# Copies inside SBUF issued from three queues by kind, the compressing products with split weights and blocks, and another order of the forget attention's projections

## The chip, the cores and the metric

One core of one Trainium2 chip runs one program, two transformer blocks one after the other. The metric is the device time of an execution in microseconds (us), as the median of several. In the text PE is TensorE, DVE VectorE, ACT ScalarE, POOL GpSimd and SP SyncE; the last three also issue DMAs, each from a queue of its own that is served in order.

## The reference, cut to what matters

512 tokens of width 1024, float32. The first block has forget attention and gated linear attention side by side, cross attention and an MLP; the second has a SwiGLU, differential attention beside a sparse attention (NSA), and another SwiGLU. What the change touches:

```python
# block 1: fq, fk, fv, ff (forget attention), gq, gk, gv, glr, gr (gated linear attention)
proj = xn @ w_in
fq, fk = rms_norm(fq per head, g_q), rms_norm(fk per head, g_k)
log_f = log_sigmoid(ff + b); c = cumsum(log_f)
p = softmax(fq.fk/8 + c_t - c_s, causal); fox_out = p @ fv
# block 2: rotary embedding on q and k of the differential attention, on q and two k of NSA
apply_rope: [x1*cos - x2*sin, x2*cos + x1*sin]
# compress(x_raw, pos, w1, w2), once for keys and once for values
blocks = x_raw[31 blocks of 32 tokens, stride 16] + pos      # (31, 2 groups, 32*64)
return gelu(blocks @ w1) @ w2                                # w1: 2048 x 256, w2: 256 x 64
```

## The kernel before, in words

Everything stands feature by token in SBUF. To keep float32 accuracy in single-pass products, a float32 matrix is split into a rounded part h (ACT, `act`, L154) and the rest l (DVE, `lo`, L148); a product is then h by h, h by l and l by h. Weights come from HBM on SP's queue into a ring of three tiles `wraw`, and are split into a ring of four tiles `wspl` (`wsub`, L176 on); `lin` makes a 512-token projection out of 24 products, `nat` one with the tokens on the partitions out of 96 products with 256 columns. The results go to PSUM tiles `lin`, of which the attention stages have three.

The score products read keys and queries twice side by side: `dup` copies the h part of the keys into a tile `kd` and the l part into `kl` (four copies of 64x512 each), and `stacks` puts h and l of the queries into `qu` (two copies of h, two of l). Such a copy is a DMA inside SBUF, `move` (L371). `rope` (L434) swaps halves of 32 partitions by four DMAs of 32x512 into a tile `tb`. In the kernel before all of them are issued from POOL's queue, where POOL's own operations also stand.

Each stage is a pair of generators, an attention and a filler (the projections that it still needs), which `weave` interleaves by the time of the products that each has issued; `pipe` lets several projections of a filler overlap, so that one goes on where another yields `LATER`. The order inside an engine is then set by the build's scheduler, by its own times. In the forget attention (`fox`, scores of 8 heads; `fox_in`) the filler was the list `[gates(), key(0), query(0), value(0), key(1), query(1), value(1)]`, and after it `gla_proj(0)`, projections of the gated linear attention. `gates()` holds the log-sigmoids, with four loads of ACT's function table, and the cumulated sums.

`cmp_in(i)` makes the blocks for the compression: a projection, four shifted copies on POOL's queue into a `wraw` tile, and two additions of the positions (DVE) into a tile `nsv`. `compress(i)` streams the weights cw1 through four `wraw` tiles and multiplies them in float32: 64 products over the two calls, 128 weights' columns by 64 columns of blocks. A float32 product is two matmul records in the trace.

Of the kernel before, what the change touches and what calls it, by code (L numbers as in the profile page):

```python
# [122 lines left out]
class Net:  # L123
    def __init__(self, tc, a, dbg=None):
        self.tc, self.nc, self.a = tc, tc.nc, a
        self.dbg = dbg or (lambda *x: None)
        self.mark = lambda n: None
        self.tb = {"d": 1}
        self.lag = 2
        self.groups = [[0], [1, 3], [2]]  # L130
        self.foxp = [None] * 4
        self.foxs = 0
        self.foxvok = [False, False]
        self.dap = [None] * 8
# [247 lines left out]
    def dup(self, t, U):  # L382

        for j in range(2):
            for r in range(2):
                self.move(U[r * 64:(r + 1) * 64, j], t[j * 64:(j + 1) * 64])
        return U
# [158 lines left out]
    def mixer(self):  # L546
# [74 lines left out]
    def fox_in(self, X, rb, rn, p1, p2, y, gate, first):  # L621
# [37 lines left out]
        K = {}  # L659

        def key(g):
            def done(t, ps):
                kh, kl = self.R(), self.R()
                self.scaled_split(ps, self.gcol("foxk"), kh, kl)
                K[2 * g + t] = [self.dup(z, p2.tile([128, 2, 512], F32R, name=n)) for z, n in ((kh, "kd"), (kl, "kl"))]
            yield from self.head_tiles(a["n_fqk"][2 + g], X, rn, p1, lambda t: self.foxs >= 2 * (2 * g + t) - 2, done,
                                       None if g else first)
# [14 lines left out]
        yield from pipe([gates(), key(0), query(0), value(0), key(1), query(1), value(1)])  # L682
# [302 lines left out]
    def mix2(self, hctx, densepsum):  # L985
# [4 lines left out]
        with ExitStack() as r0:  # L990
            with ExitStack() as l0:
                z = None
                with ExitStack() as r1:
                    with ExitStack() as l1:
# [6 lines left out]
                        with ExitStack() as c:  # L1001
# [12 lines left out]

                            def fill():
                                self.N = {}
                                pieces = [[self.nsa_key(0, X, rb, n1)], [self.nsa_key(1, X, rb, n1)],
# [100 lines left out]
    def da_key(self, h, X, rb, p2):  # L1118
# [8 lines left out]
        self.dak[h] = [self.dup(t, p2.tile([128, 2, 512], F32R, name=n)) for t, n in zip(z, ("kd", "kl"))]  # L1127
# [119 lines left out]
    def nsa_key(self, b, X, rb, p1):  # L1247
# [8 lines left out]
        for U, t in zip(self.N["kb"], (kh, kl)):  # L1256
            self.dup(t, U[:, b])
# [170 lines left out]
    def cmp_in(self, i, X, rb, p1):  # L1428

        nc, a = self.nc, self.a  # L1430
        p2 = self.tmp
        ps = yield from self.lin(a["t_c4"][i], X)
        k0 = self.T("a")
        self.tt(k0, ps, rb, OP.mult)

        B = p1.tile([128, 4, 2, 2, 2, 64], F32R, name="nsv") if i == 0 else self.Bt
        self.Bt = B
        B = B.rearrange("p a b c d e -> p (a b c d e)").bitcast(F32)[:, i * 1024:(i + 1) * 1024]
        B = B.rearrange("p (k g n) -> p k g n", k=16, g=2)
        nc.gpsimd.memset(B, 0.0)  # L1440
        pos = p2.tile([128, 16], F32, name="cpos", bufs=1)
        nc.sync.dma_start(pos, a["cpos"][i])
        sh = self.wraw.tile([128, 1024], F32, name="wraw").rearrange("p (g n) -> p g n", g=2)
        for g in range(2):
            nc.gpsimd.dma_start(sh[0:64, g], k0[64 * g:64 * g + 64])
            nc.gpsimd.dma_start(sh[64:128, g, 0:511], k0[64 * g:64 * g + 64, 1:512])
        yield LATER
        for g in range(2):

            v = bass.AP(tensor=sh.tensor, offset=sh[:, g].offset, ap=[list(sh.ap[0]), [2, 16], [16, 31]])  # L1450
            self.tt(B[:, :, g, 0:31], v, pos[:, :, None].to_broadcast([128, 16, 31]), OP.add)
        self.B = B

    def compress(self, i, p1):
# [3 lines left out]
        if True:  # L1458
            pc = None
            for c in range(4):  # L1460
                w = self.wraw.tile([128, 1024], F32, name="wraw")
                w3 = w.rearrange("p (k n) -> p k n", k=4)
                nc.sync.dma_start(w3, a["cw1"][i][:, 4 * c:4 * c + 4])
                yield LATER
                if pc is None:
                    B = self.B
                    pc = self.ps()
                    pss = [pc[:, :64], pc[:, 64:128]]
# [8 lines left out]
            nc.vector.tensor_copy(x, pc[:, :128])  # L1477
# [9 lines left out]
            r = 4 if i else 1  # L1487
            H = p2.tile([128, 2, 2, r, 32], F32, name=f"ch{i}", bufs=1)
            for m in range(2):
                self.tt(H[:, m], *(z[:, 64 * m:64 * m + 64].rearrange("p (g n) -> p g n", g=2)[:, :, None]  # L1490
                                   .to_broadcast([128, 2, r, 32]) for z in (x, u)), OP.mult)
            w2 = p2.tile([128, 2, 128], F32, name="cw2", bufs=1)
            nc.sync.dma_start(w2, a["cw2"][i])
            yield LATER
            if i == 0:
                ps = self.ps()
                for m in range(2):
                    self.mm(ps[:, :64], w2[:, m], H[:, m, :, 0], m == 0, m == 1)
# [6 lines left out]
            else:  # L1505
# [3 lines left out]
                for g in range(2):  # L1509
                    ps = self.ps()  # L1510
                    for m in range(2):
                        self.mm(ps[:, :64], H[:, m, g].rearrange("p r n -> p (r n)"), w2[:, m, :64], m == 0, m == 1)
# [173 lines left out]
```

## Time and profile before

| | |
|---|---|
| median of 3 runs | 2279.53 us (2278.78 to 2280.15) |
| profiled execution | 2278.2 us, its span 2276.4 us |
| PE busy | 2222.3 us (98%) |
| DVE, ACT, POOL busy | 1278.6, 967.3, 371.2 us (56%, 42%, 16%) |
| mean granted clock of PE | 0.983 |
| DMA mean, HBM read | 100 GB/s, 188.91 MB |

The profile describes one execution. Times are counted from the start of its span; 1.8 us of the execution lie outside it. PE is never far from busy, so what a change can win are the stretches where PE waits, and those where its granted clock is at the lower of its two levels (1.2 GHz instead of 2.4 GHz: 0.5 in the profile). The views by stretch of time show both side by side.

### The profile page before, as it was taken

The numbers are of one execution on the slowest core, as the hardware profiler recorded it, in microseconds if no ns is written. First come the engines' busy times: TensorE is split into PE (matmuls) and PEld (weight loads), VectorE is DVE, ScalarE is ACT, GpSimd is POOL, SyncE is SP. The second block draws the span as 40 slices with busy tenths as digits, with TensorE's granted clock in tenths as the row PEclk, the third lists the DMA queues.
The fourth block names the chain that finished last, engine by engine and source line by source line (L and its number), as shares of the span: only waits on it lengthen the run. The fifth ranks groups of instructions, "written<-read, shape, count | busy, mean of one in ns | idle before, by whom it ended". The sixth has DMA issues, their size and how long they took to land. (4 is left out here: it accounts for less than half of the span.)

```text
span 2276.4 us, 30717 instructions
## 1 busy us (share of the span) xinstructions
PE 2222.3 (98%) x11491; PEld 1867.7 (82%) x11491; DVE 1278.6 (56%) x2403; ACT 967.3 (42%) x1941; POOL 371.2 (16%) x569
## 2 busy tenths in 40 slices
PE   9999999999999999999999899999999999999998
PEld 8887799888888888888887788788877888888887
DVE  6565566654345444434456667778784555543543
ACT  6553455444234333323343244466675334332332
POOL 1431012100000000000005345445651000000000
PEclk9999999999999999999999899999999999999999
DMA  3441243233333333233345655512212333333322
GB/s 134 112 121 52 75 122 108 63 95 96 96 99 94 101 93 96 89 104 101 101 137 142 168 165 153 147 43 66 63 45 65 112 102 93 94 91 104 102 88 79
DMA packets 75108, 228.13 MB, mean 100 GB/s; under 512 B 12560, under 2 KB 20464, under 8 KB 74960
## 3 DMA queue, kind: packets, MB, share of 16 engines
q1 hardware_dynamic: 61392, 192.48, 27.9%
q0 software_dynamic: 12992, 33.18, 5.6%
q8 instruction: 90, 1.47, 0.3%
q14 instruction: 58, 0.48, 0.1%
q10 hardware_dynamic: 576, 0.52, 0.1%
HBM read 188.91 MB, written 4.19 MB: 85 GB/s over the span
## 5 line engine op out<-in xcount | busy, mean ns | idle before, releaser
L154 ACT ACTIVATE wspl<-wraw 128x512 fp32r<-128x512 f32 (+1 forms) x677 | 422.3, 627 | 877.6 <-PE lin L145 800.3
L148 DVE TENSOR_TENSOR wspl<-wraw,wspl 128x512 fp32r<-128x512 f32 (+1 forms) x677 | 470.0, 697 | 428.0 <-ACT wspl L154 420.8
L244 POOL TENSOR_TENSOR rqr<-rqv,mhalf 128x4 f32<-128x4 f32 (+1 forms) x21 | 20.5, 977 | 1369.2 <-DVE rqv L241 1358.6
L145 PE MATMUL lin<-x0h,wspl 128*128 128x512 f32 (+2 forms) x396 | 158.1, 400 | 2.2 <-DVE h L151 0.9
L154 ACT ACTIVATE P<-s,nm 128x128 f32<-128x128 f32 (+2 forms) x224 | 117.5, 529 | 86.1 <-DVE nm L316 73.8
L145 PE MATMUL lin<-x1h,wspl 128*128 128x512 f32 (+2 forms) x396 | 153.6, 389 | 0.0
L145 PE MATMUL lin<-x7h,wspl 128*128 128x512 f32 (+2 forms) x396 | 153.5, 388 | 0.0
L145 PE MATMUL lin<-x2h,wspl 128*128 128x512 f32 (+2 forms) x396 | 153.5, 388 | 0.0
L145 PE MATMUL lin<-x3h,wspl 128*128 128x512 f32 (+2 forms) x396 | 153.2, 388 | 0.0
L145 PE MATMUL lin<-x4h,wspl 128*128 128x512 f32 (+2 forms) x396 | 153.0, 387 | 0.0
L145 PE MATMUL lin<-x6h,wspl 128*128 128x512 f32 (+2 forms) x396 | 152.9, 387 | 0.0
L145 PE MATMUL lin<-x5h,wspl 128*128 128x512 f32 (+2 forms) x396 | 152.7, 386 | 0.0
L316 DVE TENSOR_REDUCE nm<-s 128x1 f32<-128x128 f32 (+3 forms) x208 | 105.3, 510 | 38.7 <-PE s L145 37.7
L148 DVE TENSOR_TENSOR ptl<-tr,pth 128x512 fp32r<-128x512 f32 x152 | 88.2, 597 | 19.8 <-ACT pth L154 18.6
L154 ACT ACTIVATE pth<-tr 128x512 fp32r<-128x512 f32 x152 | 74.8, 530 | 39.6 <-PE tr L342 34.6
L145 PEld LDWEIGHTS lin<-x0h,wspl 128*128 128x128 f32 (+1 forms) x396 | 75.3, 190 | 17.5 <-ACT wspl L154 3.5
L342 PE MATMUL tr<-ident,P 128*128 128x128 f32 x480 | 83.1, 283 | 4.8 <-DVE P L151 3.5
L145 PEld LDWEIGHTS lin<-x2h,wspl 128*128 128x128 f32 (+1 forms) x396 | 74.7, 189 | 15.3
L145 PEld LDWEIGHTS lin<-x1h,wspl 128*128 128x128 f32 (+1 forms) x396 | 74.9, 189 | 14.8
L145 PEld LDWEIGHTS lin<-x3h,wspl 128*128 128x128 f32 (+1 forms) x396 | 74.4, 188 | 15.2
L145 PEld LDWEIGHTS lin<-x7h,wspl 128*128 128x128 f32 (+1 forms) x396 | 74.5, 188 | 15.0 <-issue 0.3
L145 PEld LDWEIGHTS lin<-x4h,wspl 128*128 128x128 f32 (+1 forms) x396 | 74.4, 188 | 14.8
(707 smaller groups left out, 5673.2 us busy)
## 6 DMA issues: line engine op xcount, KB each, us to landing
wraw<-in_t_m SPq DMA_DIRECT2D x64, 512.0 KB, 3.8
wraw<-in_t_f1a SPq DMA_DIRECT2D x22, 512.0 KB, 3.6
wraw<-in_t_f1b SPq DMA_DIRECT2D x22, 512.0 KB, 3.5
wraw<-in_t_f2a SPq DMA_DIRECT2D x22, 512.0 KB, 3.5
wraw<-in_t_f2b SPq DMA_DIRECT2D x22, 512.0 KB, 3.5
qu<-r POOLq DMA_DIRECT2D x80, 128.0 KB, 3.1
wraw<-in_t_f1c SPq DMA_DIRECT2D x16, 512.0 KB, 3.5
wraw<-in_t_f2c SPq DMA_DIRECT2D x16, 512.0 KB, 3.5
```

The costliest lines, as they stand in the source:

```text
L145: self.nc.tensor.matmul(out, lhsT, rhs, start=start, stop=stop, **kw)
L148: self.nc.vector.tensor_tensor(out, in0, in1, op=op)
L154: self.nc.scalar.activation(out, in_, func, **kw)
L244: self.nc.gpsimd.tensor_tensor(r, v, self.mhalf[:, :m], op=OP.pow)
L316: self.nc.vector.tensor_reduce(nm, ps, axis=AX.X, op=OP.max, negate=True)
L342: self.nc.tensor.transpose(ps[:, n:n + 128], P(qb, kb) if callable(P) else P[:, self.po(qb) + kb * 128:self.po(qb) + (kb + 1) * 128], self ...
```

## The change

It does four things. `move` and `rope` get a queue by kind: copies of an h part are issued from ACT, copies of an l part from POOL as before, and the four copies of a `rope` from SP (96, 104 and 104 of the 304). The blocks of the compression are split into h and l, and its weights run through `wsub` like all others: 64 products with 128 columns (h weights by h and l of the blocks) and 64 with 64 columns (l by h), one matmul record each, and 16 more splits on ACT and DVE; the shifted copies go into tiles `tb` instead of `wraw`. In the forget attention's filler `key(0)` stands ahead of `gates()`, and `gla_proj(0)` behind `value(0)` instead of at the end. The two tiles `cpos` and `cw2` are loaded earlier, the repeated hidden vector is copied by POOL (two operations).

```diff
+        self.q = {"hi": self.nc.scalar, "lo": self.nc.gpsimd, "rope": self.nc.sync}
...
-    def move(self, dst, src):
-        self.nc.gpsimd.dma_start(dst.bitcast(F32), src.bitcast(F32))
+    def move(self, dst, src, q="lo"):
+        self.q[q].dma_start(dst.bitcast(F32), src.bitcast(F32))
...
-        self.move(U[0:64, 0], hi[0:64])
+        self.move(U[0:64, 0], hi[0:64], "hi")
         self.move(U[64:128, 0], lo[0:64])
         self.move(U[0:64, 1], lo[64:128])
-        self.move(U[64:128, 1], hi[64:128])
+        self.move(U[64:128, 1], hi[64:128], "hi")
...
         for q in range(4):
-            self.nc.gpsimd.dma_start(sw[q * 32:(q + 1) * 32], src[(q ^ 1) * 32:(q ^ 1) * 32 + 32])
+            self.q["rope"].dma_start(sw[q * 32:(q + 1) * 32], src[(q ^ 1) * 32:(q ^ 1) * 32 + 32])
...
-                yield from self.fox_in(X, rb, rn, p1, p2, y, gates, first)
-                yield from self.gla_proj(0, X, rb, rn, p0)
+                yield from self.fox_in(X, rb, rn, p1, p2, y, gates, first, self.gla_proj(0, X, rb, rn, p0))
...
-        yield from pipe([gates(), key(0), query(0), value(0), key(1), query(1), value(1)])
+        yield from pipe([key(0), gates(), query(0), value(0), other, key(1), query(1), value(1)])
...
+            t = self.T("c").rearrange("p (k n) -> p k n", k=16)
+            nc.vector.memset(t[:, :, 31:32], 0.0)
+            self.tt(t[:, :, 0:31], v, pos[:, :, None].to_broadcast([128, 16, 31]), OP.add)
+            self.act(B[:, :, 0, g], t, AF.Copy)
+            self.lo(B[:, :, 1, g], t, B[:, :, 0, g])
...
             for c in range(4):
-                w = self.wraw.tile([128, 1024], F32, name="wraw")
-                w3 = w.rearrange("p (k n) -> p k n", k=4)
-                nc.sync.dma_start(w3, a["cw1"][i][:, 4 * c:4 * c + 4])
-                yield LATER
+                W = self.wsub(a["cw1"][i][:, 4 * c:4 * c + 4])
...
-                for k in range(4):
+                for k, (h, l) in enumerate(W):
                     for m in range(2):
-                        self.mm(pss[m], w3[:, k, m * 128:(m + 1) * 128],
-                                B[:, 4 * c + k].rearrange("p g n -> p (g n)"),
-                                c + k + m == 0, c + k == 6, skip_group_check=True)
-                yield 8 * 213
+                        w, o = slice(128 * m, 128 * m + 128), 128 * m
+                        self.mm(pc[:, o:o + 128], h[:, w], B[:, 4 * c + k], c + k + m == 0, False,
+                                skip_group_check=True)
+                        self.mm(pc[:, o:o + 64], l[:, w], B[:, 4 * c + k, :64], False, c + k == 6,
+                                skip_group_check=True)
+                yield 8 * 110
```

Three places show how the order moves. Line numbers of the changed kernel are 2 higher at these helpers. **Start of the forget attention, ACT**, from the narrow gate rows on (`tc`, `td` and `cm` belong to `gates()`; `hraw` and `tb` empty a PSUM tile of `query(0)`). Before:

```order
L154 ACTIVATE tc<-tc 8x512
L154 ACTIVATE td<-s,gc 128x512
L154 ACT_TABLE_LOAD
L154 ACTIVATE tc<-tc 8x512
L154 ACTIVATE tc<-s,gc 128x512
L154 ACT_TABLE_LOAD
L154 ACTIVATE td<-td 128x512
L154 ACTIVATE tc<-tc 128x512
L154 ACT_TABLE_LOAD
L154 ACTIVATE td<-td 128x512
L154 ACTIVATE tc<-tc 128x512
L154 ACTIVATE cm<-ta 8x512
```

and now:

```order
L156 ACTIVATE tc<-tc 8x512
L156 ACT_TABLE_LOAD
L156 ACTIVATE tc<-tc 8x512
L156 ACTIVATE hraw<-lin 128x256
L156 ACTIVATE tb<-lin 128x256
L156 ACTIVATE hraw<-lin 128x256
```

One table load instead of three, and 2 other rows instead of 9, stand between the narrow gate row and the emptying of `query(0)`'s tiles; the other loads now stand among the tiles of `value(0)`, together with 8 copies of the h part of the keys.

**Start of the differential attention, PE**, at the first score products (`kd`, `kl`, `qu` of head 0). Before, behind the projection of `cmp_in(0)`:

```order
L145 MATMUL lin<-x7h,wspl 128x512
L145 MATMUL lin<-x7l,wspl 128x512
L145 MATMUL lin<-x7h,wspl 128x512
L145 MATMUL s<-kd,qu 128x128
L145 MATMUL s<-kl,qu 128x128
```

and now, after 12 products of the first `da_value`:

```order
L147 MATMUL lin<-wspl,x2h 128x256
L147 MATMUL lin<-wspl,x3h 128x256
L147 MATMUL s<-kd,qu 128x128
L147 MATMUL s<-kl,qu 128x128
L147 LDWEIGHTS identb
L147 MATMUL s<-maskb,identb 128x128
L147 MATMUL lin<-wspl,x3l 128x256
```

The first scores moved ahead of 84 products with 256 columns and 24 with 512, and the following ones lie between those products.

**The same place, SP.** Before:

```order
L180 DMA wraw<-in_t_kda 128x1024
L180 DMA wraw<-in_t_qda 128x1024
L180 DMA wraw<-in_n_vda 128x1024 x2
L180 DMA wraw<-in_t_c 128x1024
L1463 DMA wraw<-in_cw 128x1024
L180 DMA wraw<-in_t_c 128x1024
```

and now:

```order
L182 DMA wraw<-in_t_qda 128x1024
L182 DMA wraw<-in_n_vda 128x1024
L436 DMA tb<-ta 32x512 x8
L182 DMA wraw<-in_n_vda 128x1024
L436 DMA tb<-ta 32x512 x8
L182 DMA wraw<-in_t_c 128x1024
L182 DMA wraw<-in_cw 128x1024
L436 DMA tb<-ta 32x512 x8
L182 DMA wraw<-in_t_c 128x1024
```

The copies of six `rope` stand between the loads of weights that set SP's pace.

## Rows read from the trace of the kernel before

**Rows 1.** The page: busy time of the engines; the groups of weight splits.
```profile
PE 2222.3 (98%) x11491; PEld 1867.7 (82%) x11491; DVE 1278.6 (56%) x2403; ACT 967.3 (42%) x1941; POOL 371.2 (16%) x569
...
L154 ACT ACTIVATE wspl<-wraw 128x512 fp32r<-128x512 f32 (+1 forms) x677 | 422.3, 627 | 877.6 <-PE lin L145 800.3
L148 DVE TENSOR_TENSOR wspl<-wraw,wspl 128x512 fp32r<-128x512 f32 (+1 forms) x677 | 470.0, 697 | 428.0 <-ACT wspl L154 420.8
```
**Rows 2.** By stretch: us, busy of PE, PEld, DVE, ACT, POOL, granted clock, DMA.
```profile
35.00:85.00 50.00, 41.02 (x286) 38.22 (x284) 26.61 (x56) 24.52 (x55) 21.36 (x32) 0.83 0.43 111
1235.00:1285.00 50.00, 39.44 (x175) 30.98 (x175) 30.39 (x61) 15.50 (x42) 23.57 (x44) 0.80 0.57 159
1285.00:1325.00 40.00, 36.25 (x198) 28.23 (x197) 28.69 (x63) 14.58 (x38) 15.91 (x26) 0.91 0.58 158
1425.00:1485.00 60.00, 55.41 (x319) 46.58 (x318) 43.20 (x98) 29.20 (x79) 22.31 (x40) 0.94 0.48 131
1485.00:1675.00 190.00, 189.13 (x1131) 157.79 (x1131) 150.68 (x357) 121.03 (x325) 103.68 (x148) 1.00 0.22 61
1675.00:1717.00 42.00, 37.26 (x225) 29.24 (x224) 33.96 (x86) 28.80 (x85) 24.93 (x40) 0.92 0.09 20
1237.00:1250.00 13.00, 7.77 (x37) 4.61 (x35) 9.07 (x23) 6.46 (x20) 10.25 (x19) 0.84 0.62 171
```
**Rows 3.** Waits of PE from 35 to 85 us: total, times, longest.
```profile
PE s L145 <- DMA qu<-r: 5.4, 1, 5.4
PE lin L145 <- ACT tb L154: 3.4, 1, 3.4
```
**Rows 4.** Timeline of ACT in the gates: start, us, operation.
```profile
29.46 0.71 ACT L154 ACTIVATE tc<-misc,gc 8x512 f32<-8x512 f32 x1
...
31.72 1.28 ACT L154 ACT_TABLE_LOAD   x1
...
41.96 0.38 ACT L154 ACTIVATE tb<-lin 128x256 f32<-128x256 f32 x1 [1.77 <-DVE cs L653]
```
**Rows 5.** Timeline of POOL, the first copies of the forget attention.
```profile
57.98 4.17 POOL L371 DMA_DIRECT2D kd<-r  x8 [4.01 <-ACT r L154]
```
**Rows 6.** Waits of PE from 1235 to 1330 us.
```profile
PE s L145 <- ACT P L154: 2.8, 5, 1.0
PE lin L145 <- issue: 2.8, 1, 2.8
PE s L145 <- DMA qu<-r: 2.7, 1, 2.7
PE lin L145 <- DMA wraw<-in_cw: 2.2, 1, 2.2
```
**Rows 7.** Timeline of POOL at the start of the differential attention.
```profile
1203.71 4.02 POOL L434 DMA_DIRECT2D tb<-ta  x8 [8.79 <-DVE ta L151]
...
1224.87 1.10 POOL L371 DMA_DIRECT2D qu<-r  x2
```
**Rows 8.** A DMA issued on ACT; the page's issues of `qu`, us to landing.
```profile
L1553 ACTq DMA_DIRECT2D outT<-x1h x1: 381/381/381, 2269.3 to 2269.3; - x1
...
qu<-r POOLq DMA_DIRECT2D x80, 128.0 KB, 3.1
```
**Rows 9.** Timeline of PE at compressing and score products of 128 columns.
```profile
1288.44 1.67 PE L145 MATMUL lin<-nsv,wraw 128*128 128x64 f32 x14
1289.93 0.31 PE L145 MATMUL s<-kd,qu 128*128 128x128 f32 x1
1290.07 0.28 PE L145 MATMUL s<-kl,qu 128*128 128x128 f32 x1
```
**Rows 10.** Stretches with one kind of product: 512 columns; 256 columns (PE alone).
```profile
600.00:700.00 100.00, 100.00 (x443) 82.84 (x442) 40.35 (x59) 34.00 (x54) 0.00 (x0) 1.00 0.31 95
...
105.00:110.00 5.00, 5.00 (x43) 1.00 0.34 110
```
**Rows 11.** Timeline of SP: two loads, the second waiting for its buffer.
```profile
1314.73 9.37 SPq L180 DMA_DIRECT2D wraw<-in_n_vda  x2
```

More of the change, by code (lines that the diff above doesn't have):

```diff
@@ L619, in log_sigmoids, with fox_in @@
             yield m
-    def fox_in(self, X, rb, rn, p1, p2, y, gate, first):
+    def fox_in(self, X, rb, rn, p1, p2, y, gate, first, other):
         nc, a = self.nc, self.a
@@ L664, in done @@
                 self.scaled_split(ps, self.gcol("foxk"), kh, kl)
-                K[2 * g + t] = [self.dup(z, p2.tile([128, 2, 512], F32R, name=n)) for z, n in ((kh, "kd"), (kl, "kl"))]
+                K[2 * g + t] = [self.dup(z, p2.tile([128, 2, 512], F32R, name=n), q)
+                                for z, n, q in ((kh, "kd", "hi"), (kl, "kl", "lo"))]
             yield from self.head_tiles(a["n_fqk"][2 + g], X, rn, p1, lambda t: self.foxs >= 2 * (2 * g + t) - 2, done,
@@ L1013, in mix2 @@
                             d1, d2 = self.newpool("da1", 1, c), self.newpool("da2", 2, c)
+                            self.cpos = n1.tile([128, 32], F32, name="cpos")
+                            for i in range(2):
+                                nc.sync.dma_start(self.cpos[:, 16 * i:16 * i + 16], a["cpos"][i])
                             def fill():
                                 self.N = {}
+                                self.B = {}
                                 pieces = [[self.nsa_key(0, X, rb, n1)], [self.nsa_key(1, X, rb, n1)],
@@ L1126, in da_key @@
         z = self.split(k1, p2, "k", hring=True, lring=True)
-        self.dak[h] = [self.dup(t, p2.tile([128, 2, 512], F32R, name=n)) for t, n in zip(z, ("kd", "kl"))]
+        self.dak[h] = [self.dup(t, p2.tile([128, 2, 512], F32R, name=n), q)
+                       for t, n, q in zip(z, ("kd", "kl"), ("hi", "lo"))]
     def da_query(self, h, X, rb, p2):
@@ L1255, in nsa_key @@
             self.N["kb"] = [p1.tile([128, 2, 2, 512], F32R, name="kb" + x) for x in "hl"]
-        for U, t in zip(self.N["kb"], (kh, kl)):
-            self.dup(t, U[:, b])
+        for U, t, q in zip(self.N["kb"], (kh, kl), ("hi", "lo")):
+            self.dup(t, U[:, b], q)
     def nsa_gates(self, X, rb, p1):
@@ L1434, in cmp_in @@
         self.tt(k0, ps, rb, OP.mult)
[L1436 to L1443, printed above, removed]
+        sh = []
         for g in range(2):
-            nc.gpsimd.dma_start(sh[0:64, g], k0[64 * g:64 * g + 64])
-            nc.gpsimd.dma_start(sh[64:128, g, 0:511], k0[64 * g:64 * g + 64, 1:512])
+            t = self.T("b")
+            nc.gpsimd.dma_start(t[0:64], k0[64 * g:64 * g + 64])
+            nc.gpsimd.dma_start(t[64:128, 0:511], k0[64 * g:64 * g + 64, 1:512])
+            sh.append(t)
         yield LATER
+        B = p1.tile([128, 4, 2, 2, 2, 64], F32R, name="nsv")
+        B = B.rearrange("p a b c d e -> p (a b c d e)").rearrange("p (k z g n) -> p k z g n", k=16, z=2, g=2)
+        pos = self.cpos[:, 16 * i:16 * i + 16]
         for g in range(2):
-            v = bass.AP(tensor=sh.tensor, offset=sh[:, g].offset, ap=[list(sh.ap[0]), [2, 16], [16, 31]])
-            self.tt(B[:, :, g, 0:31], v, pos[:, :, None].to_broadcast([128, 16, 31]), OP.add)
-        self.B = B
+            v = bass.AP(tensor=sh[g].tensor, offset=sh[g].offset, ap=[list(sh[g].ap[0]), [2, 16], [16, 31]])
+            t = self.T("c").rearrange("p (k n) -> p k n", k=16)
[3 more added lines that the diff above has]
+            self.lo(B[:, :, 1, g], t, B[:, :, 0, g])
+        self.B[i] = B
     def compress(self, i, p1):
@@ L1458, in compress @@
         if True:
-            pc = None
+            w2 = p2.tile([128, 2, 128], F32, name="cw2", bufs=2)
+            nc.sync.dma_start(w2, a["cw2"][i])
             for c in range(4):
-                w = self.wraw.tile([128, 1024], F32, name="wraw")
-                w3 = w.rearrange("p (k n) -> p k n", k=4)
-                nc.sync.dma_start(w3, a["cw1"][i][:, 4 * c:4 * c + 4])
-                yield LATER
-                if pc is None:
-                    B = self.B
+                W = self.wsub(a["cw1"][i][:, 4 * c:4 * c + 4])
+                if c == 0:
+                    yield LATER
+                    B = self.B[i].rearrange("p k z g n -> p k (z g n)")
                     pc = self.ps()
-                    pss = [pc[:, :64], pc[:, 64:128]]
-                for k in range(4):
+                for k, (h, l) in enumerate(W):
                     for m in range(2):
-                        self.mm(pss[m], w3[:, k, m * 128:(m + 1) * 128],
-                                B[:, 4 * c + k].rearrange("p g n -> p (g n)"),
-                                c + k + m == 0, c + k == 6, skip_group_check=True)
-                yield 8 * 213
+                        w, o = slice(128 * m, 128 * m + 128), 128 * m
[4 more added lines that the diff above has]
+                yield 8 * 110
             yield LATER
             x = p2.tile([128, 128], F32, name="cx", bufs=1)
-            nc.vector.tensor_copy(x, pc[:, :128])
+            pz = pc[:, :256].rearrange("p (m z n) -> p m z n", m=2, z=2)
+            x3 = x.rearrange("p (m n) -> p m n", m=2)
+            self.act(x3, pz[:, :, 1], AF.Copy)
+            self.tt(x3, pz[:, :, 0], x3, OP.add)
             u = p2.tile([128, 128], F32, name="cu", bufs=1)
@@ L1485, in compress @@
             nc.vector.reciprocal(u, u)
[L1487 to L1493, printed above, removed]
+            H = p2.tile([128, 2, 64], F32, name="ch", bufs=1)
+            self.tt(H.rearrange("p m n -> p (m n)"), x, u, OP.mult)
             yield LATER
@@ L1510, in compress @@
                     ps = self.ps()
+                    H4 = p2.tile([128, 2, 4, 32], F32, name="cr", bufs=1)
+                    nc.gpsimd.tensor_copy(H4, H[:, :, None, 32 * g:32 * g + 32].to_broadcast([128, 2, 4, 32]))
                     for m in range(2):
-                        self.mm(ps[:, :64], H[:, m, g].rearrange("p r n -> p (r n)"), w2[:, m, :64], m == 0, m == 1)
+                        self.mm(ps[:, :64], H4[:, m].rearrange("p r n -> p (r n)"), w2[:, m, :64], m == 0, m == 1)
                     for j in range(2):
```

6 lines of the change are left out of this document (3 added, 3 removed).

## The prediction

> **What bounds the kernel now.** The page's busy row first: TensorE (PE) works 2222.3 of 2276.4 us, the next engine, VectorE, 56% [rows 1]. So the change can win only where PE is idle, 54.1 us in all, and where its granted clock lies below 1, the level of 2.4 GHz. I read the view by stretches next, around the places the change touches, and took two losses from each row: idle is length less PE's busy time, clock loss is (1 − granted clock) × busy time [rows 2]. Start of the forget attention, 35 to 85 us: 50 − 41.02 = 9.0 idle, 0.17 × 41.02 = 7.0 clock, 16.0 together. Start of the differential attention, 1235 to 1325: 10.6 + 3.75 idle, 7.9 + 3.3 clock, 25.5. Its end, 1425 to 1485: 4.6 + 3.3 = 7.9. In the sparse stage PE is idle for 0.9 us of 190. Idle time drags the clock with it: over the 90 us, 11.2 us of clock loss go with 14.3 us idle, 0.78 for each; at the start of the forget attention it is 7.0 / 9.0 = 0.78 again. I use that ratio to price waits: one microsecond of wait in these places costs 1.78.
>
> The views of waits say what ended them. Forget attention: a projection waits 3.4 us for a copy out of PSUM on ACT, a score 5.4 us for a `qu` transfer [rows 3]. Differential attention: 2.8 us on ACT's probabilities, 2.7 on `qu`, 2.2 on a cw weight, 2.8 on nothing that the profile names [rows 6]; the rest is in small pieces. The timelines show why. ACT begins the narrow gates at 29.46 and empties the next PSUM tile at 41.96, with function table loads of 1.28 us between [rows 4]. POOL spends 4.17 us on issuing eight key copies [rows 5], and issues 28 copies from 1203.71 to 1224.87 + 1.10 = 1225.97, where the last `qu` of head 0 leaves: at about 0.52 us, 14.6 of 22.3 us [rows 5, 7].
>
> **The change part by part.**
>
> *Forget attention, start.* (a) ACT's gap is 41.96 − 29.46 = 12.5 us. Three `lin` tiles of 24 products at 0.116 us (5 us / 43) [rows 10] cover 8.4 us; the missing 4.1 is about the 3.4 wait [rows 3, 4]. Now one table load and three narrow rows stand there, 1.28 + 3 × 0.71 = 3.4 us: under the cover, gone. (b) The `qu` wait. From the query's transposes to its transfer landed there are a rounding and its rest of 512 columns (the weight splits' 0.627 + 0.697 = 1.3 [rows 1]), two POOL issues (1.1) and 3.1 us to land [rows 7, 8]: 5.5 us. Behind them stood 15 products of 256 columns, 1.7 us; now 3 of 512 and 40 of 256, 3 × 0.226 + 40 × 0.116 = 5.3 [rows 10]. Left: about 0.3. (c) New: three table loads (3.8), six gate rows of full width (6 × 0.63 = 3.8) and eight issues on ACT, at 0.381 [rows 8] 3.0, now stand among the emptying of `value(0)`: 10.7 us plus the emptying itself (3 us), 13.7 against some 13 us of products, with weight splits queued behind on ACT. I charge 3 us idle. Left (0.3 + 3) × 1.78 = 5.9 of 16.0: **gain 10.1**, bounds 16 and 0.
>
> *Forget attention, end.* `gla_proj(0)` was its last filler. Without it 14 score blocks, 40 transposes and 37 value products, about 18 us of PE work by their spacing, run alone. The trace has two stretches of attention alone. From 1237 to 1250, 5.2 us idle and 1.2 of clock are lost on 6.5 us of work at full clock (7.77 × 0.84), ratio 1.0; from 1675 to 1717, 7.7 on 34.3, ratio 0.22 [rows 2]. The first is the beginning of an attention, where the pipeline is still empty; here, as in the second, it runs full and drains. I take 0.22: **cost 4.0**, bounds 0 and 18.
>
> *Differential attention, start.* Of the 28 issues POOL keeps six (four `kl`, two `qu`), so 22 × 0.52 = 11.4 us leave the chain in front of the last one: 1225.97 − 11.4 + 3.1 = 1217.7 for head 0's operands [rows 7, 8]. The first scores stood at 1237.6 and now come ahead of 84 × 0.116 + 24 × 0.226 = 15.2 us of filler [rows 10]: 1222.4. So they should not wait, and those 15.2 us of projections lie between scores which ran alone from 1237 to 1250. The wait for cw falls as well: those loads waited for free `wraw` tiles that the products themselves held; now the splits free them. Of 14.3 us idle I keep the 2.8 of no name and half of the 5.9 that are in no named row: 2.8 + 3.0 = 5.8, with the clock 10.3. **Gain 15.2**, bounds 23 (only 1.4 idle left) and 5 (only the waits on cw and half a microsecond more go). What pays for it: 16 more splits cost 16 × 0.627 = 10.0 us on ACT and 11.2 on VectorE, which were busy 30 and 59 of these 90 us [rows 1, 2]; if that cover fails, up to 11 us come back. An issue on ACT follows its source on the same engine, so it waits only where a `kd` or `qu` tile isn't free yet, with exponentials and splits queued behind; before, the issues of `kd` waited for ACT or nothing [rows 5], so I cost that at 0 beyond its 0.381.
>
> *The compressing products.* Before, 128 records at 0.106 (1.49 us / 14) [rows 9], 13.6 us. Now 64 with 128 columns and 64 with 64. A score product of 128 columns starts 0.14 us after the one before [rows 9], one of 256 takes 0.116: between 0.057 (half of 256) and 0.14 for the wide ones, and for the narrow ones between 0.03 and 0.106. By bounds 5.6 to 15.7 us; I take 0.116 and 0.106, nearest rows in size, 14.2: **cost 0.6**, bounds −8 and +2.
>
> *End of the differential attention* (7.9 us lost). It ends as before, with fewer issues on POOL: **gain 2**, bounds 6 and 0. *Sparse stage*: POOL loses 48 issues (25 of its 104 us), ACT takes 16, 6.1 us on 121 of 190; 0.9 us is idle: **0**, ±3. The other moves (earlier `cpos` and `cw2`, two copies on POOL) are single operations off the path.
>
> *SP's queue.* 26 ropes come to stand among weight loads, 104 issues. If the source is ready, a group of eight costs SP some 3 us of issuing, in a queue where a load stood 9.37 us waiting for its buffer [rows 11]: SP runs ahead of PE by more than that. **0**; the price if it isn't so is a rival below.
>
> Sum: 10.1 − 4.0 + 15.2 − 0.6 + 2 = 22.7. From the profiled execution, 2278.2 (span 2276.4, 1.8 outside), that gives 2255.5; the median stands 1.3 higher, so **2256.8 us**.
>
> **The rivals.** A: *issuing is not the price, transfer is.* Both `qu` waits stay, because the transfers share the same DMA engines with more copies begun at once. For it: 0.57 to 0.62 of the DMA engines' time is taken between 1235 and 1325, the highest of the stretches [rows 2]. Against: head 0's 28 issues take 14.6 us of POOL, a landing 3.1. Of 5.4 + 2.7 only 0.3 was kept, so 7.8 × 1.78 = 13.9 comes back: 2270.7.
> The Trainium skill ("DMA: Bandwidth & Descriptors", "Issuing engines are not separate DMA queues") speaks against the change here: whichever engine begins a DMA, it runs on the same 16 engines, and several issuers save only the sequencer's time, usually small beside the DMA. By that rule rival A's time would come; the rows of POOL show issues that add up to more than a landing, so for these small copies the trace so far disagrees.
>
> B: *the uncovered end of the forget attention is like 1237 to 1250.* Cost 18 in place of 4: 2270.8. For it: the same kind of softmax chain through ACT and VectorE. Against: many heads' scores were already ahead.
>
> C: *SP becomes the bound* (slower). A rope waits in SP's queue for VectorE's result, and every weight load behind it waits too; or it waits behind a load that has no buffer, 9.37 us in one row [rows 11], and the key comes late. The price is 26 × x. From x = 0.87 us it eats the gain; at 1.5 us it takes 39: 2295.8. For it: such rows, and the ring of only three tiles. Against: a load has its slack in the same number, and the order places ropes after loads that run ahead.
>
> D: *the waits only move.* PE's 98% leaves little, and scores that start earlier wait later for probabilities: 2279.5.
>
> **How the numbers follow.** Forecast 0.64, A 0.11, B 0.09, C 0.10, D 0.06. The range should leave out two in ten: C's core and D (0.16), and the ends of the forecast. It goes down to 2242 (differential start at 23 and sparse and end terms at their better bounds, or forget start at 16) and up to 2275, which holds A and B. What a measurement of this kernel can tell from no change is 0.2%, 4.6 us, so faster means below about 2275: 0.61 of the forecast's 0.64, 0.16 of the 0.20 of A and B, 0.01 of C: 0.78. Within 0.2%: 0.02 of the forecast, 0.04 of A and B, 0.01 of C, 0.04 of D: 0.11. Slower: 0.11, 0.08 of it C, 0.02 D and 0.01 the forecast.
>
> **What would show it.** Right: in the waits of the forget attention's start both rows are gone or under 1 us, and the stretch of 50 us loses some 6 us; at its end, behind the last product of `value(1)`, PE loses about 4 us; the scores of the differential attention begin while projections go on, with idle time under 7 us over the same work and the granted clock near 1; the compressing records number 128 as before; POOL's busy time falls by the 200 issues that leave it, about 104 us. Wrong: PE waiting for `wspl` splits that wait for `wraw` loads behind a rope (C); a `qu` wait of several microseconds with POOL idle (A); ACT standing at a copy's issue for a free `kd` or `qu` tile, with exponentials behind it; more than 8 us of loss at the end of the forget attention (B).

## The result and the profile after

The changed kernel takes 2262.02 us (median of 6 executions, 2252.91 to 2267.77); before, measured beside it, 2279.16. The ratio is 0.9926, 95% interval 0.9902 to 0.9951: 11 to 22 us faster. 2256.8 had been forecast, range 2242 to 2275. The profiled execution took 2262.6 us, its span 2260.8.

The stretches that answer to each other begin and end at the same products: the start, the first product on `y6h` (linear attention), the first of block 2's projections, the first score of the sparse attention (`kcT`), the sums behind that attention, the last transposes. Columns: start and end, us, busy time of PE, granted clock, DMA share, GB/s. Before:

```profile
0.00:266.27 266.27, 253.65 (x1652) 0.96 0.34 100
266.27:1185.63 919.36, 915.52 (x4344) 1.00 0.32 99
1185.63:1475.03 289.40, 271.27 (x1567) 0.95 0.55 153
1475.03:1762.09 287.06, 278.89 (x1622) 0.98 0.21 58
1762.09:2268.00 505.91, 502.54 (x2307) 1.00 0.32 96
2268.00:2276.40 8.40, 0.41 (x2) 0.50 0.38 125
```

After:

```profile
0.00:259.10 259.10, 249.76 (x1652) 0.99 0.35 103
259.10:1176.88 917.78, 913.90 (x4345) 1.00 0.32 99
1176.88:1462.51 285.63, 272.14 (x1566) 0.95 0.57 157
1462.51:1743.37 280.86, 274.01 (x1623) 0.99 0.20 57
1743.37:2248.90 505.53, 502.16 (x2307) 0.99 0.31 96
2248.90:2260.80 11.90, 0.39 (x2) 0.50 0.27 90
```

So of the 15.6 us by which the profiled span is shorter the forget attention's stretch brings 7.2, the differential attention's 3.8, the sparse one's 6.2; 2.0 come from the long projections, and the program's end takes 3.5 back. The forecast had 6.1 for the first, 16.6 for the second (compressing products and end included) and 0 for the third. Split another way, the 15.6 us are 5.7 of idle time of PE, 7.3 of clock loss (half of PE's busy time at granted clock 0.5) and 2.6 fewer busy microseconds at full clock.

Waits of PE at the two places [rows 3, 6], after; first 30 to 200 us:

```profile
PE tr L424 <- DVE r L153: 1.5, 1, 1.5
PE lin L147 <- ACT wspl L156: 1.2, 1, 1.2
PE o L147 <- DVE yt L150: 1.1, 2, 0.9
```

and 1180 to 1330 us:

```profile
PE lin L147 <- DVE tc L1458: 4.3, 1, 4.3
PE tr L344 <- DVE P L153: 2.5, 1, 2.5
PE s L147 <- ACT P L156: 1.9, 2, 1.1
PE s L147 <- DMA qu<-r: 1.5, 2, 1.0
```

In the first place the waits of 5.4 and 3.4 us are gone. In the second the wait for cw and the nameless one are gone and the `qu` wait is smaller. The wait for VectorE's `P` is not new: it took 3.1 us before, the longest row there, which [rows 6] leave out. New is the one of 4.3 us for VectorE. The timelines of SP, ACT, VectorE and PE show what it is (start, us, operation, in brackets the idle time before it and what ended it):

```profile
1213.50 8.22 SPq L436 DMA_DIRECT2D tb<-ta  x8
1233.48 15.69 SPq L182 DMA_DIRECT2D wraw<-in_cw  x3
...
1237.18 1.62 ACTq L373 DMA_DIRECT2D kd<-r  x1
...
1245.91 0.69 DVE L150 TENSOR_TENSOR r<-tc,r 128x512 fp32r<-128x512 f32 x1 [4.99 <-DMA kd<-r]
1246.52 0.68 DVE L150 TENSOR_TENSOR ta<-lin,rstdb 128x512 f32<-128x512 f32 x1
...
1247.86 0.80 PE L147 MATMUL lin<-x0h,wspl 128*128 128x512 f32 x1 [4.31 <-DVE tc L1458]
```

VectorE is to write the query's low part over a tile `r` that a `kd` copy still reads. Until that copy has landed everything behind stands, the emptying of a `lin` tile too, and PE with it. The view of the tile `kd` from 1215 to 1250 gives the landings, and the view by stretch the reason (us, PE, PEld, DVE, ACT, POOL, granted clock, DMA share, GB/s):

```profile
DMA to landing us min/median/max: 2.3/5.4/8.6
...
1236.00:1240.00 4.00, 4.00 (x19) 3.32 (x18) 1.76 (x5) 1.56 (x4) 1.95 (x4) 1.00 0.84 211
1240.00:1244.00 4.00, 3.06 (x18) 1.90 (x16) 0.88 (x2) 2.12 (x4) 0.00 (x0) 1.00 1.01 238
```

From 1240 to 1244 us all DMA engines are full: `kd`, `kl` and `qu` copies, begun from two queues at once, run there with loads of cw.

### The profile page after: what moved, and what is told of

It is laid out like the page before. It is cut to its first block, busy times and chain, and to the rows that moved or that the text cites. A ratio compares the mean times of both kernels' runs of the same rounds, so it can differ in the third digit from the quotient of the medians.

```text
span 2260.8 us, 30847 instructions
## 1 busy us (share of the span) xinstructions
PE 2212.4 (98%) x11491; PEld 1861.7 (82%) x11491; DVE 1280.6 (57%) x2425; ACT 979.7 (43%) x1963; POOL 266.9 (12%) x369
## 3 DMA queue, kind: packets, MB, share of 16 engines
q0 software_dynamic: 5056, 13.77, 2.4%
## 4 chain that ended last, share of the span: by engine, by line
PE 91%; DVE 3%; DMA 2%; ACT 2%; issue 1%; ACTq 1%; SPq 0%; DVEq 0%; POOL 0%; POOLq 0%
PE lin L147 78%; PE s L147 6%; PE o L147 4%; PE tr L344 2%; PE tr L147 2%; DMA kd<-r 1%; ACTq L373 1%; DVE nm L318 0%; DVE tc L150 0%; ACT P L156 0%; DVE ptl L150 0%; DMA kbh<-r 0%; DVE wspl L150 0%; ACT tb L156 0%; DMA wraw<-in_t_qda 0%
## 5 line engine op out<-in xcount | busy, mean ns | idle before, releaser
L156 ACT ACTIVATE wspl<-wraw 128x512 fp32r<-128x512 f32 (+1 forms) x693 | 432.1, 626 | 866.8 <-PE lin L147 801.0
L150 DVE TENSOR_TENSOR wspl<-wraw,wspl 128x512 fp32r<-128x512 f32 (+1 forms) x693 | 476.0, 690 | 417.1 <-ACT wspl L156 407.6
```

Source lines behind the costliest of these rows:

```text
L150: self.nc.vector.tensor_tensor(out, in0, in1, op=op)
L156: self.nc.scalar.activation(out, in_, func, **kw)
```

## The experiments

Three parts can be had apart: the queues by kind (Q), the forget attention's order (F), the compressing products (C). Idle is length less PE's busy time; clock loss is half of PE's busy time in the spells at granted clock 0.5. Both are of the one profiled execution, in the stretch up to the linear attention and in that from block 2 to the sparse scores. The runs stand on three chips, each beside the kernel before, whose medians there were 2276.94, 2276.39 and 2277.59 us; the last three rows and changed_again share one.

| run | parts | ratio to before, interval | first stretch: idle, clock | differential: idle, clock |
|---|---|---|---|---|
| before | none | 1 | 12.6, 7.8 | 18.1, 10.9 |
| queue_alone | Q | 0.9970 (0.9958 to 0.9983) | 14.6, 4.9 | 14.6, 8.8 |
| order_alone | F | 0.9988 (0.9978 to 0.9997) | 11.5, 4.8 | 16.0, 12.4 |
| compress_alone | C | 0.9985 (0.9977 to 0.9994) | 12.0, 7.0 | 15.9, 11.8 |
| order_compress | F, C | 1.0000 (0.9990 to 1.0010) | 11.2, 4.7 | 19.4, 10.5 |
| queue_order | Q, F | 0.9943 (0.9931 to 0.9955) | 9.3, 3.1 | 16.3, 9.5 |
| queue_compress | Q, C | 0.9966 (0.9949 to 0.9982) | 14.3, 11.5 | 12.6, 5.1 |
| changed kernel | Q, F, C | 0.9926 (0.9902 to 0.9951) | 9.3, 1.7 | 13.5, 14.9 |
| changed_again | Q, F, C | 0.9931 (0.9916 to 0.9947) | 8.9, 1.7 | 12.7, 13.0 |
| high_on_act | F, C, h from ACT | 0.9982 (0.9970 to 0.9993) | 8.9, 8.5 | 19.8, 13.2 |
| rope_on_sp | F, C, ropes from SP | 0.9912 (0.9898 to 0.9926) | 11.4, 4.8 | 9.7, 8.6 |
| rope_on_act | F, C, ropes from ACT | 0.9962 (0.9947 to 0.9976) | 11.8, 3.4 | 15.9, 10.5 |
| fox_high | F, C, ropes SP, h ACT early | 0.9888 (0.9868 to 0.9908) | 9.0, 5.1 | 8.9, 9.4 |
| fox_high_fp32 | F, ropes SP, h ACT early | 0.9883 (0.9866 to 0.9900) | 9.6, 5.1 | 11.8, 6.0 |

**Queues alone.** The kernel before with this:

```diff
+        self.q = {"hi": self.nc.scalar, "lo": self.nc.gpsimd, "rope": self.nc.sync}
```

and the calls of `move`, `dup` and `rope` that use it.

> The kernel before with only the queues by kind (h copies from ACT, ropes from SP). Theory 1, the sum of the prediction: POOL's issues were the price of the two qu waits, 5.4 us in the forget attention and 2.7 us in the differential attention; with the clock that goes with them, 1.78 for each us, some 8 to 14 us are gained, ratio 0.994 to 0.9965, and POOL has 200 issues fewer. Theory 2 (rival A): the transfers share the DMA engines; the copies land no earlier than before (kd 2.8, qu 3.1 us in the kernel before, kd 4.2 and ACT's qu 3.4 in the changed one), the waits stay and the time is within 0.2% of before. Theory 3 (rival C): loads behind ropes on SP make it slower by over 0.2%.

The median was 2269.98 beside 2276.94: 7 us, just short of theory 1. PE's waits from 30 to 190 us:

```profile
PE lin L147 <- ACT tb L156: 3.4, 1, 3.4
PE s L147 <- DMA qu<-r: 2.1, 1, 2.1
```

The 5.4 us wait falls to 2.1; the wait for ACT's copy, not a matter of queues, stays. Three new waits, 3.5 us together, stand beside them (for VectorE's `r` and for ACT's splits), and the first stretch is as long as before, 266.2 us: the gain lies in block 2. The first scores of the differential attention begin 36.9 us behind block 2's start instead of 51.9. Theory 3 falls: SP does not become the bound.

**Order alone.**

```diff
-        yield from pipe([gates(), key(0), query(0), value(0), key(1), query(1), value(1)])
+        yield from pipe([key(0), gates(), query(0), value(0), other, key(1), query(1), value(1)])
```

> The kernel before with only the new order of the forget attention's projections. Theory 1: it takes the 3.4 us wait (terms a) and most of the 5.4 us wait (term b) by itself, since 43 products now stand behind the query's transposes, and gives back 4 us at the end of that attention; ratio 0.996 to 0.998, the first 266 us shorter by 5 to 9 us, block 2 unchanged. Rival: without the queue split POOL's eight key copies stand ahead of the two qu copies, so the 5.4 us wait stays, the end costs 4 us, and the ratio is 0.999 to 1.001.

Measured 0.9988, between the two. Both waits go without any new queue, as theory 1 had it with term (b), the 43 products behind the query's transposes. But the first stretch is shorter by 1.9 us only. From 150 to 190 us PE waits, where before there was filler:

```profile
PE s L145 <- ACT P L154: 2.6, 5, 1.3
PE o L145 <- DVE yt L148: 1.1, 2, 0.9
PE o L145 <- ACT pth L154: 0.7, 2, 0.5
```

and a spell of half clock came with it (158 to 165 us, 3.1 us lost).

**Compressing products alone.**

```diff
-                w = self.wraw.tile([128, 1024], F32, name="wraw")
-                nc.sync.dma_start(w3, a["cw1"][i][:, 4 * c:4 * c + 4])
+                W = self.wsub(a["cw1"][i][:, 4 * c:4 * c + 4])
```

> The kernel before with only the split compressing products (and the earlier loads of cpos and cw2). Theory 1: the wait of 2.2 us for a cw weight goes, with its clock 4 us, and the products take 3 us less of PE (the changed kernel has 3 us less PE work at full clock in that stretch): ratio 0.9965 to 0.9985. Rival: the 16 more splits and the blocks' splits on VectorE and ACT cost what the waits gave, and the 4.3 us wait of the changed kernel for VectorE (its product after 1243 us) comes with this part: ratio 0.999 to 1.002.

Measured 0.9985: theory 1 at its smallest gain. The wait for cw is gone. The products themselves cost the same: in the trace the fp32 records start 0.112 us apart, the new ones 0.143 (128 columns) and 0.081 (64), 14.3 us either way. The 4.3 us wait does not come with this part; its scores still begin 54.9 us behind the block's start.

**Order and products, all copies on POOL.** The changed kernel with

```diff
-        self.q = {"hi": self.nc.scalar, "lo": self.nc.gpsimd, "rope": self.nc.sync}
+        self.q = {"hi": self.nc.gpsimd, "lo": self.nc.gpsimd, "rope": self.nc.gpsimd}
```

> The changed kernel with all copies back on POOL's queue (order and compressing products changed). Theory 1: without the queue split the differential attention keeps its qu wait (2.7 us) and POOL 200 more issues: about 5 to 8 us slower than the changed kernel, ratio to before 0.995 to 0.997. Theory 2 (rival A): equal to the changed kernel, ratio 0.991 to 0.994, and the 4.3 us wait behind a copy of kd that takes 8.6 us to land stays as long, since the DMA engines are full there (share about 1.0 from 1240 to 1244 us). If it is the issue from ACT that delays that copy, this wait is gone here.

Exactly the time of before, outside what either theory expected: the two small gains don't add up. In the differential attention the scores now wait for ACT and VectorE, by the view of waits from 1190 to 1340 us:

```profile
PE s L145 <- ACT P L154: 9.7, 12, 1.8
PE tr L342 <- DVE P L151: 5.6, 5, 1.5
```

The 4.3 us wait is not there. The whole value of the change, 0.9926 to 0.9931, hangs on the queues in this company. Theory 2 (rival A) falls.

**Queues and order.** The changed kernel with `compress` and `cmp_in` as before.

> The changed kernel with the compressing products as before (queues and order changed). With the queues alone block 2 up to the sparse scores took 281.5 us, with the whole change 285.6. Theory 1: the gain comes from queues and order together, and the compressing products give nothing once the copies land early; the time is that of the changed kernel or 2 to 5 us less, ratio 0.990 to 0.993, the forget attention's start like the changed kernel's (no qu wait), the 4.3 us wait for VectorE absent. Rival: the compressing part carries its 3 us of PE work and the cw wait (1.7 us with the queues alone) in every company: ratio 0.994 to 0.996.

2264.18 us, 0.9943: the rival's value by the medians, the split products are worth 0.0012 to 0.0017 there; but the interval overlaps those of the changed kernel (0.9926 and 0.9931), so that this is not clear of the noise.

**Queues and products.** The changed kernel with the old list `[gates(), key(0), ...]`.

> The changed kernel with the forget attention's old order (queues and compressing products changed). Theory 1: the 3.4 us wait for ACT's copy and about 2 us of the qu wait come back, 7 us more than the changed kernel up to the first 266 us: ratio 0.995 to 0.997. Rival: what the order gains at the start it gives back at its end (order alone moved that stretch by 1.9 us only): ratio 0.992 to 0.994.

0.9966, theory 1: the 3.4 us wait is back. The first stretch is 272.3 us long, 13.2 more than in the changed kernel where 7 had been expected; 4.9 of it is idle time, 9.8 clock. Something else shows here. From block 2's start to the sparse scores the instructions of all five engines stand in the same order in this kernel and in the changed one. Yet it took 275.7 us here, 285.6 there: idle 12.6 and 13.5, clock 5.1 and 14.9. At the products of the second `compress`, changed kernel:

```profile
1282.00:1294.60 12.60, 12.29 (x76) 1.00 0.67 184
1294.60:1311.70 17.10, 17.10 (x68) 0.50 0.63 196
```

and this one, at the same products:

```profile
1293.52:1305.72 12.20, 12.20 (x76) 1.00 0.68 183
1305.72:1315.05 9.33, 9.20 (x67) 1.00 0.81 240
```

The same products take 17.1 us at half clock there and 9.3 us here.

**Ropes or h copies.** Two runs with one of the two queues back on POOL:

```diff
-        self.q = {"hi": self.nc.scalar, "lo": self.nc.gpsimd, "rope": self.nc.sync}
+        self.q = {"hi": self.nc.gpsimd, "lo": self.nc.gpsimd, "rope": self.nc.sync}
```

> The changed kernel with the h copies back on POOL and only the ropes on SP. Order and compressing products alone gave 1.000, the whole change 0.9926. Theory 1: the ropes' issues were what held POOL ahead of the differential attention (16 of 28), so its first scores come nearly as early as in the changed kernel (36.7 us behind the block's start, against 54.9 with all on POOL) and half or more of the gain is there: ratio 0.994 to 0.996; without the kd copies on ACT the 4.3 us wait for VectorE behind a kd copy is shorter or as long. Rival: the h copies are the lever, ratio 0.998 to 1.000.

```diff
-        self.q = {"hi": self.nc.scalar, "lo": self.nc.gpsimd, "rope": self.nc.sync}
+        self.q = {"hi": self.nc.scalar, "lo": self.nc.gpsimd, "rope": self.nc.gpsimd}
```

> The changed kernel with the ropes back on POOL and only the h copies on ACT. Theory 1: the forget attention, which has no ropes, is as in the changed kernel (259 us up to the linear attention's projection), and the differential attention gets a third of its gain, first scores some 45 us behind the block's start: ratio 0.995 to 0.998. Rival: copies on ACT hold up its probabilities and splits, ratio 0.999 or more.

The ropes alone give 2258.11 us, 0.9912, all that the whole change gives and more than theory 1 had; the h copies alone 0.9982, between theory 1 and the rival, with the first scores 53.1 us behind the block's start and not 45. Their first stretch took 265.1 us where 259 had been expected; its idle time, 8.9 us, is that of the changed kernel, its clock loss 8.5 us against 1.7. The same stretch with the ropes alone, and with the h copies alone (columns as in the first fence):

```profile
1183.50:1458.20 274.70, 264.95 (x1567) 0.96 0.58 161
```

```profile
1182.80:1473.10 290.30, 270.48 (x1568) 0.94 0.56 151
```

With the h copies on ACT PE is idle for 19.8 us there, with the ropes on SP for 9.7. The first scores begin 44.7 us behind the block's start with the ropes on SP, 8 later than in the changed kernel: an early first score is not the whole. What VectorE waited for from 1190 to 1340 us, changed kernel:

```profile
DVE wspl L150 <- ACT wspl L156: 12.1, 11, 3.2
DVE r L150 <- DMA kd<-r: 9.8, 3, 5.0
```

and with the ropes alone:

```profile
DVE wspl L150 <- ACT wspl L156: 14.9, 14, 3.0
...
DVE r L150 <- DMA kd<-r: 1.2, 1, 1.2
```

The waits for `kd` copies fall from 9.8 to 1.2 us. The 9.8 is one execution: in changed_again the row has 5.2, in queue_compress, with the same order, 4.8, and the wait of PE behind it 3.5 and 3.1 in place of 4.3. Wherever the h copies of this stretch come from POOL and the ropes do not, the row has at most 2.7. At full clock (length less clock loss) the stretch took 270.8, 269.9 and 270.6 us in the three executions with h from ACT, 266.1 with the ropes alone and 265.4 in fox_high below: the h copies on ACT cost some 4.7 us here. Taking them off ACT moved more than this wait, so the runs show which queue is better, and this wait as the largest difference on VectorE, not as the only one. In the first stretch it is the other way round. There are no ropes, and with the new order PE is idle for 8.9 to 9.6 us in the six profiles with h from ACT, for 11.2 to 11.8 in the four with h from POOL.

**The changed kernel again, and three beside it on one chip.**

> The changed kernel itself, to stand on the same chip as the three beside it. Expected again 0.9915 to 0.994; its executions should differ by more than 10 us between them as they did (2252.9 to 2267.8), with the mean granted clock, since the old order of the forget attention with the same order of TensorE in the differential attention took 275.7 us there and this kernel 285.6, of which 9.8 us is clock.

2261.38 us, 0.9931. Executions spread over 8.7 us (2257.24 to 2265.96), a little less than expected; the two ends had granted clocks of 0.992 and 0.986.

```diff
             weave(self.fox(Y, y, p2), fill(), 5)
+            self.q["hi"] = self.nc.gpsimd
```

> The changed kernel with the h copies on ACT in the forget attention alone; later ones go from POOL, ropes from SP as in the change. Theory: the h copies on ACT help the forget attention (its stretch at full clock, idle and work, 257.4 us against 259.4 with them on POOL) and hurt the differential one, where VectorE waited 9.8 us for kd copies to land and no such wait stood in the run with the h copies on POOL (270.8 against 266.1 us at full clock). Both gains together: 2 to 6 us less than with the ropes alone, ratio 0.988 to 0.9915 and faster than the changed kernel. Rival: the h copies on ACT do nothing measurable either way, the difference between the two runs (0.9926 and 0.9912) being the clock: ratio 0.991 to 0.9935, equal to the changed kernel beside it.

2253.20 us, 0.9888, below the changed kernel's interval beside it, as the theory has it; of the 8.2 us between the two medians 3.9 lie at the program's end, where no such copy is issued (last section). Against the ropes alone, 0.9912 on another chip, the intervals overlap: that the h copies on ACT help the forget attention is seen in its idle time, not in the whole time. Idle is 9.0 and 8.9 us in the two stretches, so that each keeps the better of its two values.

The same line in the kernel whose compressing products are as before:

> The same with the compressing products as before. Theory: the split products are worth what they were in the company of queues and order (0.9926 against 0.9943), some 3 to 4 us: ratio 0.0015 above the run beside it. Rival: once the scores start early and the kd copies no longer hold VectorE, the wait for cw weights is covered and the split is worth nothing: the two equal within 0.001.

2251.06 us, 0.9883: the rival by the medians. The intervals of the two runs, four executions each, leave room for the theory's 0.0015 too. No gain from the split is seen here, and by its median this is the fastest kernel of the study, 0.5% below the changed one.

```diff
-        self.q = {"hi": self.nc.scalar, "lo": self.nc.gpsimd, "rope": self.nc.sync}
+        self.q = {"hi": self.nc.gpsimd, "lo": self.nc.gpsimd, "rope": self.nc.scalar}
```

> The changed kernel with the ropes issued from ACT and the h copies from POOL. It tells whether taking the ropes off POOL is what counts or putting them on SP. Theory: off POOL counts; 104 issues of 0.38 us on ACT cost ACT 40 us in a block where it is busy a third of the time, but its queue holds probabilities and splits behind each rope that waits for VectorE's result: 0.992 to 0.995, between the ropes on SP (0.9912) and on POOL (0.998 to 1.000). Rival: a rope's waiting source blocks ACT as it does not block SP: 0.997 or more.

2268.78 us, 0.9962, between theory and rival: better than on POOL, half as good as on SP. The first scores begin as early as with SP (44.4 us), but PE is idle for 15.9 us in place of 9.7. Over the whole stretch it waits 6.8 us for probabilities from ACT (4.5 with the ropes on SP) and 2.9 us for a `qu` copy (none). ACT itself stands for 17.8 us until a rope's copy has landed, with splits and probabilities next in its order:

```profile
ACT r L156 <- DMA tb<-ta: 7.0, 1, 7.0
...
ACT P L156 <- DMA tb<-ta: 4.8, 2, 2.8
```

With the ropes on SP no such row stands. So both count: that the ropes leave POOL, and that they don't go to an engine whose queue holds the attention's own work.

## Why the prediction was right, and where not

**Right in sign and, within its range, in size**: 17 us by medians (2279.16 − 2262.02), 22.7 forecast from the profile, where 15.6 came. That the time stayed within the range is in part luck: the differential attention fell 12.8 us short, and the sparse stage, put at 0, and the long projections, which the sum leaves out, brought 8.2. POOL's busy time fell by 104.3 us, as forecast. By terms:

- *Forget attention, start*, 10.1 forecast. Both waits went, by the covers that were counted; order_alone shows that they go by the order alone. From 30 to 80 us the changed kernel is idle for 1 us at full clock, where 3.3 had been charged: too cautious.
- *Forget attention, end*, cost 4.0, from the ratio 0.22 of the sparse stage's end. The idle time behind the last filler (133 to 180 us) is 4.5 us in the changed kernel at full clock, 1.1 about the same place before. Rival B (18 us) is out. Net 7.2 against 6.1: 3.3 of idle time and 6.1 of clock less, and 2.2 us more busy time at full clock for the same 1652 products, which the prediction did not have.
- *Differential attention*, 15.2 + 2 − 0.6 forecast, 3.8 in the profile. **This is the step that failed.** The forecast is some 9.6 us of idle time less and 7.5 of clock; measured are 4.6 of idle time less, 3.9 of clock loss more, and 3.0 fewer busy microseconds at full clock. The sum kept 5.8 us of idle time over 1235 to 1325 and let the rest go. (Its 5.9 us in no named row are 3.8 by [rows 6], 14.3 − 10.5; with them it would have kept 4.7.) The wait for cw and the nameless one did go, and the scores came 15 us earlier as worked out (36.7 behind block 2's start against 51.9). What had been costed at nothing is the landing: `kd` copies landed in 4.2 us in place of 2.8 (medians), up to 8.6 where the DMA engines were full, and VectorE stood behind them for 9.8 us (5.2 and 4.8 in the other two executions of this order), which gave PE its 4.3 us wait. The prediction looked for what an issue on ACT waits for, not for who waits for its source to come free. An issue of `kd` on ACT also took 0.61 us at the median, not 0.381. Second, and larger in this profile, the 0.78 us of clock per idle us is no price: 14.9 with 13.5, 13.0 with 12.7 and 5.1 with 12.6 were measured for one order of instructions. In these three executions the stretch gained 3.8, 6.5 and 13.7 us, so the clock alone moves this term by 10 us.
- *Compressing products*, cost 0.6: nothing, 14.3 us either way. The two prices taken were off in opposite directions (0.116 against 0.143, 0.106 against 0.081). The splits' 10 us stayed covered.
- *Sparse stage*, 0 ± 3 forecast, 6.2 in the profile: 3.4 of it clock, 1.3 idle, 1.5 fewer busy microseconds at full clock. That stretch took 280.7 to 282.9 us in all eight kernels whose ropes leave POOL, for SP or for ACT, and 285.7 to 287.1 in the five whose ropes stay, with the h copies on ACT (286.4) or not. So the short stretch goes with the ropes, not with the h copies. How they shorten it is open: in rope_on_sp all of it is clock (loss 0 in place of 6.4, idle 9.6 in place of 8.2), in rope_on_act it is idle time, clock and busy time together.
- *SP's queue*, 0, rival C: right. Eight rope issues held SP for 8.22 us from 1213.50 on, where some 3 had been estimated, and PE's waits for splits of weights in the changed kernel are 0.5 us from 1180 to 1330. In the fastest kernel of the study they are 7.1 us from 1180 to 1340 us, the largest wait there; whether ropes ahead of those loads have to do with it was not tried.

**Rival A** was half right. The Trainium skill ("DMA: Bandwidth & Descriptors", "Issuing engines are not separate DMA queues") says that issuers share the 16 engines and save only the sequencer's time, usually small beside the DMA. The sharing is in the rows: share 1.01 and slower `kd` landings. One issue is small here too, 0.50 us for a rope from POOL that lands after 3.9; what is not small is their sum ahead of a waiting product: taking the 104 rope issues of 64 KB off POOL is worth 0.9912 against 1.0000. An issue is not cheaper elsewhere (medians: a rope 0.58 us on SP, 0.60 on ACT), so the gain is not in the single issue. Left open is the kind of queue: the page has POOL's copies in q0, software_dynamic (12992 packets before, 5056 after), those of SP and ACT in q1 and q10, hardware_dynamic, and a rope landed after 2.3 us from SP (4.0 from ACT). No run here separates that from the order in the queues.

By the six runs with one or two parts and the two whole ones, Q changes the ratio by −0.0030 alone, −0.0019 beside C, −0.0045 beside F and −0.0074 beside both; C by −0.0015, −0.0004 beside Q, +0.0012 beside F. Each of these differences is uncertain by 0.002 to 0.003, so that those of C are within the noise; the spread of Q's is not. The parts don't add up; what one is worth depends on what else is late.

## What to carry to other kernels

Small copies that an engine issues one after the other are a cost of that engine's queue, and can be moved to a queue that runs ahead; choose it by stage, since for the h copies ACT was the better queue in the forget attention, by its idle time, and the worse one in the differential attention. When a copy is begun earlier, look at who waits for its source to come free, and at the DMA share of the moment. Try each part of such a change alone and left out: here one of three showed no gain in the best company, and one of the moved kinds of copies took back part of what another had won (0.9931 with the later h copies on ACT, 0.9888 without, about half of it at the program's end).

## What the runs showed that was not expected

- One order of instructions gave 5.1 and 14.9 us of clock loss in one stretch. In both profiles of the changed kernel a spell of 17.1 us at half clock stood at nearly the same products, in the first behind 12.6 us in which PE had been busy for 12.3; the same products ran at full clock in queue_compress. So a profile's clock loss is not given by the order of a stretch alone, and the executions of the changed kernel, 2252.91 to 2267.77 us, go with mean clocks from 0.992 to 0.985.
- The stretch behind the last transposes took 8.4 us before, 8.3 or 8.4 in the three runs with all copies on POOL, 11.7 to 11.9 in those with the three queues, 9.8 with the ropes alone moved, to SP or ACT, 10.5 with the h copies alone, and 7.8 in the two fastest. Its work is the same; what differs is the last long DRAIN of POOL, which the other engines await. Why it takes longer was not tried, but up to 4 us between two kernels are this and nothing of the attentions. Its time in ns is the third figure behind the count (before, changed kernel, fox_high):

```profile
L1682 POOLq DRAIN  x3: 46/98/6756, 2268.9 to 2276.1; - x3
L1693 POOLq DRAIN  x3: 46/98/10187, 2249.8 to 2260.5; - x3
L1694 POOLq DRAIN  x3: 40/102/6186, 2245.6 to 2252.3; - x3
```
